# The first pair of tiles in eight plain block products, with the weight sums made meanwhile

## The chip, the cores and the metric

One Trainium2 chip, one core. The metric is the device time of one execution in microseconds, as the median of several runs. Lower is better.

## The reference

A layer of an encoder on x of 2048 rows by 1024 columns: RMS norm, a gated linear attention mixer, residual, RMS norm, a gated convolutional feed-forward part, residual, final norm, all in float32.

```python
h = rmsnorm(x, mix_norm_w)
proj = h @ w_in                       # q, k, v, r, and 16 columns glr
q, k, v, r, glr = split(proj)
log_a = log_sigmoid(glr @ w_gate2 + b_gate) / 16
# chunks of 64 rows: state = state * decay + k_decayed^T v ; o = q state
o = rms_normalize(o) * gla_norm_w * silu(r)
x = x + o @ w_out
h = rmsnorm(x, ffn_norm_w)
u = causal_dwconv(h @ w_up, conv_w, conv_b); g, val = split(u)
x = x + (silu(g) * val) @ w_down
return rmsnorm(x, final_norm_w)
```

The change touches the start of `h @ w_in`: the 1024 columns of r (called "R" in the kernel) and the gate's 16 columns glr, for the first two row tiles.

## The kernel before

**Numbers.** A float32 operand a is held as a rounded high part and a remainder, a = hi + lo (`split`: a ScalarE cast at L185 makes hi, a VectorE subtraction at L186 makes lo). A product takes three matmuls (L178 to L180): hi·lo, lo·hi, hi·hi.

**Tiles.** The rows are taken in pairs of tiles, 2 x 128 rows. For a pair j and a group of 1024 weight columns ("R", then "A", "B", "Y"), `unit` computes a 2 x 2 block product: rows b(e), b(d), each in two halves of 512 along the inner dimension, times four weight blocks of 512 x 512. It does so with seven products instead of eight (the Strassen-Winograd scheme): p1, p5, p6, p7, p4, p2, p3. Each is 4 inner steps x 3 matmuls = 12 matmuls of 128 x 512. Weight blocks (i, j) are named by column half i and inner half j. p5 takes the sum of blocks (1,0) and (1,1), p6 that sum minus (0,0), p7 (0,0) minus (1,0), p3 (0,1) minus p6's sum; p1, p4 and p2 take (0,0), (1,1) and (0,1). On the row side, p5, p6, p7 and p4 take differences of the pair's blocks (`ht` tiles, made by `diff`). The split weights stay in tiles `w_R_p1` and so on for all eight pairs.

**A row tile's way.** `load_x` (SyncE's queue), `norm_x` (ScalarE square into `junk`, VectorE variance `var_a`, GpSimd power `rstd_a`, VectorE scaling), `blocks_x` (eight transposes on TensorE into two banks `pt_a`, two copies into `hb`), differences, split, store to DRAM (`h1d`) for the later groups.

**Order.** Each engine runs its instructions in the order in which the code issues them. The host code keeps a clock (`adv`) that products advance; `later_do(us, fn)` and the list `wevents` issue work when that clock passes a time. For the first pair the order was written out: the table `WEARLY` says how many weight products are prepared before product i, and `limit` how many rows. All sums and splits of weights for p1 to p3 are issued inside the first pair's `unit`, each ahead of its product. The blocks (0,0), (1,0) and (1,1) come by `stage_w` into tiles that later hold split weights, block (0,1) by ScalarE's queue into tiles `wr`.

**The gate.** `gate_weights` loads the 16 gate columns (`graw`), the second gate matrix and the bias (`w2raw`, eight small loads) on ScalarE's queue and splits them on VectorE (`wg`, `w2s`). `gate_mm` adds the gate's matmuls (into `pg`) to four of the seven products.

**Banks.** The eight PSUM banks are two pools of four: "mm" (products, `pg`) and "aux" (transposes and others). A tile of a pool waits until the last reader of the bank that it gets has ended.

Of the kernel before, what the change touches and what calls it, by code (L numbers as in the profile page):

```python
# [20 lines left out]
def f32(ap):  # L21
    return ap.bitcast(F32)
# [3 lines left out]
def hybrid_kernel(  # L26
# [48 lines left out]
    TB0, TB1, TB2 = 4.0, 10.0, 3.0  # L75
    TX0, TX = (16.4, 18.6), (10.8, 13.5)

# [158 lines left out]
    WSUM = ("p5", "p6", "p7", "p3")  # L236
    wgot, wload, staged = {}, {}, {}

# [41 lines left out]

    def stage_w(ps_, o, ijs):

        t = uh.tile([P, KT, 512], F32, tag=o, name=f"ws_{ps_}_{o}", bufs=1)
        for n, ij in enumerate(ijs):
            for c, src in w_block(ps_, *ij):
                nc.sync.dma_start(t[:, n * HK:(n + 1) * HK, c:c + src.shape[-1]], src)
            staged[ij] = t[:, n * HK:(n + 1) * HK, :]

    def raws_of(ps_, o, k):
        v = (slice(None), slice(2 * k, 2 * k + 2))  # L290
        return v, [wgot[ps_, o, k, ij] if (ps_, o, k, ij) in wgot else staged[ij][v] for ij in WSRC[o]]

    def sum_w(ps_, o, k):

        v, r = raws_of(ps_, o, k)
        src = xsum[v]
        if o == "p5":
            nc.vector.tensor_add(src, *r)
        elif o == "p6":
            nc.vector.tensor_sub(src, src, r[0])  # L300
        elif o == "p7":
            nc.vector.tensor_sub(r[1], *r)
        elif o == "p3":
            r = wgot[ps_, "p2", k, (0, 1)] if (ps_, "p2", k, (0, 1)) in wgot else staged[0, 1][v]
            nc.vector.tensor_sub(src, r, src)
# [91 lines left out]
    def blocks_x(t):  # L397
        xt = xin.pop(t)
        bs = []
        for k in range(2):  # L400
            pt = aux_ps(f"pt_a{t}_{k}")
            for i in range(HK):
                kt = HK * k + i
                nc.tensor.transpose(pt[:, i * P:(i + 1) * P], xt[:, kt * P:(kt + 1) * P], ident)
            b = hb_tile(f"hb_{t}_{k}")
            nc.vector.tensor_copy(b, pt)
            bs.append(b)
        hsrc["t", t] = bs
        j = t // 2
        if t % 2 == 0:  # L410
            hsrc[j, "p1"], hsrc[j, "p2"] = bs
            return
# [51 lines left out]
    def gate_weights():  # L464

        GR = 2 * RANK
        rp["wg"] = wg = rp["p"].tile([P, 2, KT, GR], F32R, name="wg")
        graw = rp["p"].tile([P, 512], F32, tag="s2k", name="graw", bufs=SB)
        gv = graw[:, :KT * RANK].rearrange("p (a b) -> p a b", b=RANK)
        nc.scalar.dma_start(gv, wv[:, :, OR + H * DV:OR + H * DV + RANK])  # L470
        nc.gpsimd.memset(f32(wg[:, 1, :, RANK:GR]), 0.0)
        nc.vector.tensor_copy(wg[:, 0, :, :RANK], gv)
        nc.vector.tensor_copy(wg[:, 1, :, :RANK], gv)
        nc.vector.tensor_sub(wg[:, 0, :, RANK:GR], gv, f32(wg[:, 0, :, :RANK]))


        rp["w2s"] = w2s = rp["p"].tile([P, 512], F32R, name="w2s")
        w2raw = rp["p"].tile([P, 512], F32, tag="s2k", name="w2raw", bufs=SB)
        for i in range(6):
            nc.scalar.dma_start(w2raw[i * RANK:(i + 1) * RANK, :], w_gate2)  # L480
        for i in range(2):
            nc.scalar.dma_start(w2raw[96 + i:97 + i, :], b_gate)
        nc.vector.tensor_copy(w2s[0:98, :], w2raw[0:98, :])
        for r in (slice(64, 96), slice(96, 98)):
            nc.vector.tensor_sub(w2s[r, :], w2raw[r, :], f32(w2s[r, :]))
        nc.vector.tensor_copy(w2s[96:97, :], w2raw[96:97, :])
        rp["gstk"] = rp["p"].tile([P, T], F32R, name="gstk")
        nc.gpsimd.memset(f32(rp["gstk"][96:98, :]), 1.0)

    def gate_mm(j, o, hh, hl):  # L490
# [17 lines left out]
        if o == "p3":  # L508
            sl = slice(j % 2 * 256, j % 2 * 256 + 256)
            g = rp["gstk"]  # L510
            nc.scalar.copy(g[0:GR, sl], pg[:GR, :256])
            nc.vector.tensor_sub(g[GR:2 * GR, sl], pg[:GR, :256], f32(g[0:GR, sl]))
            nc.scalar.copy(g[2 * GR:3 * GR, sl], pg[:GR, :256])
            ready.add(f"g{j}")
            if j % 2 == 1:
                gates(j // 2, TB0, TB1, TB2)

# [339 lines left out]
    ux = {}  # L857
    WEARLY = [0, 2, 3, 4, 5, 6, 7, 7]

    def limit(ps_, j, i):  # L860

        own = (PS.index(ps_) * NP + j + 1) * len(PORD)
        n = own - len(PORD) + i + 1 + LEAD
        if ps_ == "R" and j == 0 and i < len(PORD) - 2:
            return min(n, i + 2)
        if ps_ == "R" and j + 1 < NP:
# [3 lines left out]
    def unit(ps_, j):  # L870
# [5 lines left out]
        bank, keep = {}, {}  # L876
        first = ps_ == "R" and j == 0
        if ps_ == "R":
            if first:
                wload[ps_] = len(WHALF) - 2  # L880
                load_w(ps_, len(WHALF))
            elif j + 2 < NP:
                for t in (e + 4, d + 4):
                    xin[t] = load_x(t, "x")
            if j + 1 < NP:
                for i, t in enumerate((e + 2, d + 2)):
                    norm_x(t)
                    later_do((TX0 if first else TX)[i], lambda t=t: blocks_x(t))

# [388 lines left out]
    masks()  # L1278
    nc.gpsimd.memset(halo, 0.0)
# [123 lines left out]
```

## Time and profile before

| | |
|---|---|
| median of 3 runs | 2235.53 us (2234.98 to 2243.4) |
| profiled execution | 2241.04 us, span 2238.9 us |
| TensorE busy | 2126.9 us, 95% of the span |
| VectorE, ScalarE, GpSimd busy | 73%, 49%, 33% |
| TensorE busy, 0 to 26 us | 4.37 us |
| VectorE busy, 26 to 61 us | 32.91 us of 35 |
| second pair starts on TensorE | 60.87 us |
| third pair starts on TensorE | 86.27 us |

Busy time is summed over instructions; an idle time stands with the event that ended it. The trace's rows give start, length, engine, line, operation, output and inputs, all in microseconds from the span's start. PE is TensorE, PEld its weight load, DVE VectorE, ACT ScalarE, POOL GpSimd, SP SyncE; a q behind the name is the engine's queue of DMA issues.

### The profile page before, as it was taken

Reading aid. Unit: us, or ns where it says so; the run is one execution under the profiler, and the core shown is the slowest. Engines: PE = TensorE matmul, PEld = TensorE weight load, DVE = VectorE, ACT = ScalarE, POOL = GpSimd, SP = SyncE. Lnnn points to the kernel's source line nnn. Section 1 sums busy time; section 2 is a strip of 40 time slices with the busy share of each in tenths; the row PEclk is TensorE's granted clock in tenths of the full one; section 3 lists DMA queues with packets and bytes.
Section 4 is the critical chain, followed back from the end, with each engine's and each line's share of the span. In section 5 each row is a group of like instructions: output and inputs, shape, how many; then the busy total and the mean of one; then the engine's idle time right before and its main releaser. Section 6 shows DMA issues by size and latency. Waiting matters only on the chain.

```text
span 2238.9 us, 29122 instructions
## 1 busy us (share of the span) xinstructions
PE 2126.9 (95%) x9948; PEld 1741.8 (78%) x9948; DVE 1642.1 (73%) x2175; ACT 1107.5 (49%) x2020; POOL 729.1 (33%) x602
## 2 busy tenths in 40 slices
PE   5999999989999899899999999999999999999998
PEld 3788787877887787677787778788888888888886
DVE  7755777788778765388999787797877777557564
ACT  4554655565555576445445444444444543333342
POOL 1000111112111000265566565466655535046100
PEclk9999999999999999999999999999999999999999
DMA  6545684369546799943535428624242468454443
GB/s 209 195 156 185 206 294 126 123 198 325 169 160 196 266 318 335 364 137 123 189 127 163 147 90 282 192 76 136 71 141 71 136 230 321 137 183 151 141 171 116
DMA packets 305077, 411.78 MB, mean 184 GB/s; under 512 B 23694, under 2 KB 160062, under 8 KB 304928
## 3 DMA queue, kind: packets, MB, share of 16 engines
q1 hardware_dynamic: 266156, 346.72, 46.6%
q10 hardware_dynamic: 38772, 63.20, 8.4%
q8 instruction: 78, 1.28, 0.2%
q14 instruction: 71, 0.58, 0.1%
HBM read 266.70 MB, written 143.13 MB: 183 GB/s over the span
## 4 chain that ended last, share of the span: by engine, by line
PE 62%; DVE 14%; DMA 9%; issue 5%; ACT 5%; POOL 3%; SPq 1%; ACTq 0%; DVEq 0%; POOLq 0%
PE pd_p L179 5%; PE pd_p L180 5%; PE pd_p L178 5%; PE ua L178 5%; PE ua L179 5%; PE ua L180 5%; DVE t L1078 4%; PE mp_R L178 2%; PE uc L178 2%; PE uc L180 2%; PE uc L179 2%; PE mp_R L179 2%; PE mp_R L180 2%; DVE uw_p L186 2%; PE mp_A L178 1%
## 5 line engine op out<-in xcount | busy, mean ns | idle before, releaser
L178 PE MATMUL ua<-h_p,uw_p 128*128 128x512 f32 x704 | 280.4, 398 | 24.3 <-ACT c L1060 24.3
L179 PE MATMUL ua<-h_p,uw_p 128*128 128x512 f32 x704 | 278.9, 396 | 0.0
L180 PE MATMUL ua<-h_p,uw_p 128*128 128x512 f32 x704 | 278.5, 396 | 0.0
L1078 DVE SCALAR_TENSOR_TENSOR t<-u,cw,t 128x1024 f32<-128x1024 f32 x176 | 264.2, 1505 | 8.6 <-ACT t L1076 7.5
L179 PE MATMUL pd_p<-dw_p,da 128*128 128x512 f32 x616 | 240.1, 390 | 1.1 <-DVE da L186 1.1
L180 PE MATMUL pd_p<-dw_p,da 128*128 128x512 f32 x616 | 239.9, 389 | 0.0
L178 PE MATMUL pd_p<-dw_p,da 128*128 128x512 f32 x616 | 239.9, 389 | 0.0
L186 DVE TENSOR_TENSOR uw_p<-ur,uw_p 128x512 fp32r<-128x512 f32 x176 | 168.4, 973 | 59.4 <-ACT uw_p L185 52.3
L186 DVE TENSOR_TENSOR da<-da_p,da 128x512 fp32r<-128x512 f32 x154 | 135.6, 933 | 100.5 <-ACT da L185 99.4
L185 ACT CAST da<-da_p 128x512 fp32r<-128x512 f32 x154 | 85.2, 619 | 203.8 <-PE pd_p L180 149.9
L178 PEld LDWEIGHTS ua<-h_p,uw_p 128*128 128x128 f32 x704 | 134.3, 191 | 58.1 <-ACT c L1060 28.6
L185 ACT CAST uw_p<-us 128x512 fp32r<-128x512 f32 x132 | 82.1, 622 | 164.5 <-POOL us L1040 114.1
L186 DVE TENSOR_TENSOR uw_p<-us,uw_p 128x512 fp32r<-128x512 f32 x132 | 122.4, 936 | 53.4 <-ACT uw_p L185 53.0
L180 PEld LDWEIGHTS ua<-h_p,uw_p 128*128 128x128 f32 x704 | 134.2, 191 | 29.9
L179 PEld LDWEIGHTS ua<-h_p,uw_p 128*128 128x128 f32 x704 | 134.4, 191 | 29.4
L178 PE MATMUL uc<-h_p,uw_p 128*128 128x512 f32 x352 | 138.4, 393 | 0.7 <-DMA h_p<-hd_p 0.7
L179 PE MATMUL uc<-h_p,uw_p 128*128 128x512 f32 x352 | 138.1, 392 | 0.0
L180 PE MATMUL uc<-h_p,uw_p 128*128 128x512 f32 x352 | 138.1, 392 | 0.0
L179 PEld LDWEIGHTS pd_p<-dw_p,da 128*128 128x128 f32 x616 | 115.7, 188 | 25.9 <-DVE da L186 1.9
L1076 ACT ACTIVATE t<-u,cw 128x1024 f32<-128x1024 f32 x88 | 109.7, 1247 | 50.9 <-DVE u L1169 43.0
L178 PEld LDWEIGHTS pd_p<-dw_p,da 128*128 128x128 f32 x616 | 115.7, 188 | 24.2
L180 PEld LDWEIGHTS pd_p<-dw_p,da 128*128 128x128 f32 x616 | 115.7, 188 | 23.7
(251 smaller groups left out, 5477.8 us busy)
## 6 DMA issues: line engine op xcount, KB each, us to landing
ur<-in_ffn_w_up_dram SPq DMA_DIRECT2D x168, 256.0 KB, 3.7
da_p<-ad_p SPq DMA_DIRECT2D x154, 256.0 KB, 3.8
h_p<-hd_p SPq DMA_DIRECT2D x56, 512.0 KB, 7.6
ad_p<-as_p SPq DMA_DIRECT2D x88, 256.0 KB, 2.5
ad_p<-t SPq DMA_DIRECT2D x66, 256.0 KB, 3.2
x<-in_x_dram SPq DMA_DIRECT2D x32, 512.0 KB, 4.9
ch<-in_ffn_w_down_dram SPq DMA_DIRECT2D x61, 256.0 KB, 4.0
hr_A_p<-h1d_p SPq DMA_DIRECT2D x56, 256.0 KB, 2.7
```

The costliest lines, as they stand in the source:

```text
L178: nc.tensor.matmul(ps_ap, ah, bl, start=(first and i == 0), stop=False, **kw)
L179: nc.tensor.matmul(ps_ap, al, bh, start=False, stop=False, **kw)
L180: nc.tensor.matmul(ps_ap, ah, bh, start=False, stop=(last and i == len(pairs) - 1), **kw)
L185: nc.scalar.copy(hi, src)
L186: nc.vector.tensor_sub(lo, src, f32(hi))
L1076: nc.scalar.activation(t, u[:, 2:2 + TS], AF.Identity, scale=cw[:, 2, c:c + 1], bias=cw[:, 3, c:c + 1])
L1078: nc.vector.scalar_tensor_tensor(t, u[:, k:k + TS], cw[:, k, c:c + 1], t, op0=ALU.mult, op1=ALU.add)
```

## The change

The first pair of "R" no longer goes through `unit`. A new function `first_pair` computes it as eight plain products (2 column halves x 2 row tiles x 2 inner halves, 96 matmuls instead of 84), each of which needs only a weight block as it comes and a row block as it is transposed. Results are accumulated in four banks and copied out by ScalarE. The sums for p5, p6, p7 and p3 are issued during these products and used by the second pair first. The pair's own row differences, which only later groups read, are issued 22 us of the host clock later. The copies of the transposes of tiles 2 and 3 go from VectorE to ScalarE. The gate's loads go from ScalarE's queue to SyncE's, behind the weight blocks, and its split of `w2raw` comes 44 us of the host clock later. `wgot` replaces the staged blocks, and `stage_w`, `WEARLY` and the special cases of the first pair are removed.

```diff
-    TX0, TX = (16.4, 18.6), (10.8, 13.5)
+    TX = (10.8, 13.5)
...
 def blocks_x(t):
-            b = hb_tile(f"hb_{t}_{k}")
-            nc.vector.tensor_copy(b, pt)
+            if t < 2:
+                b = rp["p"].tile([P, 512], F32, tag="s2k", name=f"hb_{t}_{k}", bufs=SB)
+            else:
+                b = hb_tile(f"hb_{t}_{k}")
+            (nc.scalar.copy if t in (2, 3) else nc.vector.tensor_copy)(b, pt)
...
 def gate_weights():
-        nc.scalar.dma_start(gv, wv[:, :, OR + H * DV:OR + H * DV + RANK])
+        nc.sync.dma_start(gv, wv[:, :, OR + H * DV:OR + H * DV + RANK])
...
+    def gate_weights2():
-            nc.scalar.dma_start(w2raw[i * RANK:(i + 1) * RANK, :], w_gate2)
+            nc.sync.dma_start(w2raw[i * RANK:(i + 1) * RANK, :], w_gate2)
...
+        later_do(44.0, parts)
...
+    def first_pair():
...
+        fetch((0, 0), (1, 0))
+        gate_weights()
+        xin[2], xin[3] = load_x(2, "x"), load_x(3, "x")
+        fetch((1, 1))
+        gate_weights2()
+        for t in range(2):
+            norm_x(t)
+            blocks_x(t)
...
+        def sum5():
+            for k in range(2):
+                nc.vector.tensor_add(s_[V[k]], a21[V[k]], a22[V[k]])
+            split_sum("p5", [s_[V[k]] for k in range(2)])
+        def sum6():
+            for k in range(2):
+                nc.vector.tensor_sub(s_[V[k]], s_[V[k]], a11[V[k]])
+            for k in range(2):
+                nc.vector.tensor_sub(xsum[V[k]], a11[V[k]], a21[V[k]])
+            split_sum("p6", [s_[V[k]] for k in range(2)])
+        def sum7():
+            for k in range(2):
+                nc.vector.tensor_sub(a12[k], a12[k], s_[V[k]])
+            split_sum("p7", [xsum[V[k]] for k in range(2)])
...
+        def product(i, jj, k):
+            if jj == 0:
+                bank[i, k] = (aux_ps if (i, k) == (1, 1) else mm_ps)(f"m{i}{k}_{ps_}_{j}")
+            (hh, hl), (wh, wl) = h[jj, k], w[i, jj]
...
+            mm3p(bank[i, k], pairs, first=(jj == 0), last=(jj == 1))
+            if jj == 1:
+                t = out_tile(f"o{i}{k}_{ps_}_{j}")
+                nc.scalar.copy(t, bank[i, k])
+                nc.sync.dma_start(rd[k][i], t)
+        weight("p1", (0, 0), "p1")
+        row(0, 0)
+        row(0, 1)
+        weight("p3", (1, 0))
+        product(0, 0, 0)
+        gate_plain(j, 0, 0, *h[0, 0])
+        row(1, 0)
+        product(0, 0, 1)
+        gate_plain(j, 0, 1, *h[0, 1])
+        weight("p4", (1, 1), "p4")
+        row(1, 1)
+        for k in range(2):
+            r = raw_tile([P, 2, 512], f"wr_{ps_}_{k}")
+            load_block(nc.scalar, r, ps_, k, (0, 1))
+            a12.append(r)
+        need_raw[0, 1] = a12
+        product(1, 0, 0)
+        norm_x(2)
+        norm_x(3)
+        product(1, 0, 1)
+        weight("p2", (0, 1), "p2")
+        product(1, 1, 0)
+        gate_plain(j, 1, 0, *h[1, 0])
+        blocks_x(2)
+        blocks_x(3)
+        product(1, 1, 1)
+        gate_plain(j, 1, 1, *h[1, 1])
+        done["rows"] = len(PORD)
+        prep_rows(len(PORD) + 1)
+        sum5()
+        product(0, 1, 0)
+        prep_rows(len(PORD) + 2)
+        sum6()
+        product(0, 1, 1)
+        later_do(22.0, diffs)
+        for t in (4, 5):
+            xin[t] = load_x(t, "x")
+        heapq.heappush(wevents, (clock["now"] + 1.0, next(seq), sum7))
+        heapq.heappush(wevents, (clock["now"] + 5.0, next(seq), lambda: split_sum("p3", a12)))
...
-    gate_weights()
...
-    stage_w("R", "p2", ((0, 0), (1, 0)))
-    stage_w("R", "p3", ((1, 1),))
-    xin[2], xin[3] = load_x(2, "x"), load_x(3, "x")
-    for t in range(2):
-        norm_x(t)
-        blocks_x(t)
+    first_pair()
...
-        for j in range(NP):
+        for j in range(int(ps_ == "R"), NP):
             unit(ps_, j)
```

What stands where in the built program, at the places that matter. A row gives line, operation, output and inputs with their buffer numbers, and shape; `x2` means two such rows. The number after `x_`, `hb_` or `pt_a` is the row tile; `ws_p7` is the staged block (0,0), `ws_p6` blocks (1,1) and (1,0); `w_R_p1` and `w_R_p3` hold, in the first pair of the changed kernel, the split blocks (0,0) and (1,0).

SyncE's queue at the start. Before:

```order
L377 DMA x_0_537<-in_x_dram 128x1024
L1270 DMA nw_mix_539<-in_mix_norm_w_dram 128x1024
L377 DMA x_1_541<-in_x_dram 128x1024
L286 DMA ws_R_p2_543<-in_gla_w_in_dram 128x4x512 x2
L286 DMA ws_R_p3_546<-in_gla_w_in_dram 128x4x512
L377 DMA x_2_548<-in_x_dram 128x1024
L377 DMA x_3_550<-in_x_dram 128x1024
```

SyncE's queue at the start. After:

```order
L369 DMA x_0_514<-in_x_dram 128x1024
L1420 DMA nw_mix_516<-in_mix_norm_w_dram 128x1024
L369 DMA x_1_518<-in_x_dram 128x1024
L899 DMA ws_p7_520<-in_gla_w_in_dram 128x2x512 x2
L899 DMA ws_p6_521<-in_gla_w_in_dram 128x2x512 x2
L467 DMA graw_527<-in_gla_w_in_dram 128x8x16
L369 DMA x_2_533<-in_x_dram 128x1024
L369 DMA x_3_535<-in_x_dram 128x1024
L899 DMA ws_p6_521<-in_gla_w_in_dram 128x2x512 x2
L479 DMA w2raw_540<-in_gla_w_gate2_dram 16x512 x6
L481 DMA w2raw_540<-in_gla_b_gate_dram 1x512 x2
```

The weight blocks come in half blocks, and the gate's loads, which stood first on ScalarE's queue, now stand here behind them.

VectorE, from its first instruction behind the gate's first casts. Before:

```order
L483 CAST w2s_521<-w2raw_522 98x512
L485 TENSOR_TENSOR w2s_521<-w2raw_522,w2s_521 32x512
L485 TENSOR_TENSOR w2s_521<-w2raw_522,w2s_521 2x512
L206 TENSOR_SCALAR var_a0_555<-ssq_a0_553 128x1
L486 CAST w2s_521<-w2raw_522 1x512
L386 SCALAR_TENSOR_TENSOR x_0_537<-x_0_537,rstd_a0_557,nw_mix_539 128x1024
L206 TENSOR_SCALAR var_a1_577<-ssq_a1_575 128x1
L186 TENSOR_TENSOR w_R_p1_636<-ws_R_p2_543,w_R_p1_636 128x1024
L386 SCALAR_TENSOR_TENSOR x_1_541<-x_1_541,rstd_a1_579,nw_mix_539 128x1024
L406 COPY hb_0_0_565<-pt_a0_0_560 128x512
```

VectorE, from the norm of tile 0. After:

```order
L378 SCALAR_TENSOR_TENSOR x_0_514<-x_0_514,rstd_a0_556,nw_mix_516 128x1024
L378 SCALAR_TENSOR_TENSOR x_1_518<-x_1_518,rstd_a1_578,nw_mix_516 128x1024
L186 TENSOR_TENSOR w_R_p1_608<-ws_p7_520,w_R_p1_608 128x1024 x2
L186 TENSOR_TENSOR w_R_p3_620<-ws_p6_521,w_R_p3_620 128x1024
L469 CAST wg_526<-graw_527 128x8x16
L470 CAST wg_526<-graw_527 128x8x16
L471 TENSOR_TENSOR wg_526<-graw_527,wg_526 128x8x16
L186 TENSOR_TENSOR w_R_p3_620<-ws_p6_521,w_R_p3_620 128x1024
L955 TENSOR_TENSOR xsum_507<-ws_p7_520,ws_p6_521 128x1024 x2
L401 COPY hb_0_0_564<-pt_a0_0_559 128x512
```

The `w2s` steps are gone from here (they stand behind the sum for p5 now), and the first copy of a transposed block stands behind four weight splits and the difference for p7.

ScalarE, around the end of the first pair (`o` tiles are results, `m` and `mp` banks of products). Before:

```order
L974 COPY o21_R_0_805<-mp1_R_0_656 128x512
L204 ACTIVATE junk_5_927,ssq_a5_928<-x_5_887 128x1024
L185 CAST w_R_p3_809<-xsum_507 128x1024 x2
L185 CAST h_R1_p1_853<-hb_2_0_824 128x512
L185 CAST h_R1_p5_881<-ht_1_p5_847 128x512
```

After:

```order
L185 CAST w_R_p5_821<-ws_p7_520 128x1024 x2
L185 CAST w_R_p6_849<-ws_p7_520 128x1024 x2
L185 CAST w_R_p3_948<-wr_R_0_681 128x1024
L985 COPY o10_R_0_744<-m10_R_0_685 128x512
L401 COPY hb_2_0_760<-pt_a2_0_755 128x512
L401 COPY hb_2_1_767<-pt_a2_1_762 128x512
L401 COPY hb_3_0_774<-pt_a3_0_769 128x512
L401 COPY hb_3_1_781<-pt_a3_1_776 128x512
L185 CAST h_R1_p1_815<-hb_2_0_760 128x512
```

The copies of tiles 2 and 3 now stand on ScalarE behind the casts for p5, p6 and the first half of p3.

More of the change, by code (lines that the diff above doesn't have):

```diff
@@ L279, in make_sums @@
             later_do(8.0 + 3.0 * i, lambda st=st: step(*st))
[L281 to L287, printed above, removed]
     def raws_of(ps_, o, k):
         v = (slice(None), slice(2 * k, 2 * k + 2))
-        return v, [wgot[ps_, o, k, ij] if (ps_, o, k, ij) in wgot else staged[ij][v] for ij in WSRC[o]]
+        return v, [wgot[ps_, o, k, ij] for ij in WSRC[o]]
     def sum_w(ps_, o, k):
@@ L508, in gate_mm, with gate_rows @@
         if o == "p3":
[L509 to L516, printed above, removed]
+            gate_rows(j)
+    def gate_rows(j):
+        GR = 2 * RANK
+        pg = rp["pg"]
+        sl = slice(j % 2 * 256, j % 2 * 256 + 256)
+        g = rp["gstk"]
+        nc.scalar.copy(g[0:GR, sl], pg[:GR, :256])
+        nc.vector.tensor_sub(g[GR:2 * GR, sl], pg[:GR, :256], f32(g[0:GR, sl]))
+        nc.scalar.copy(g[2 * GR:3 * GR, sl], pg[:GR, :256])
+        ready.add(f"g{j}")
+        if j % 2 == 1:
+            gates(j // 2, TB0, TB1, TB2)
     def gates(b, t0, t1, t2):
@@ L876, in unit @@
         bank, keep = {}, {}
-        first = ps_ == "R" and j == 0
         if ps_ == "R":
[L879 to L882, printed above, removed]
+            if j + 2 < NP:
                 for t in (e + 4, d + 4):
@@ L887, in unit @@
                     norm_x(t)
-                    later_do((TX0 if first else TX)[i], lambda t=t: blocks_x(t))
+                    later_do(TX[i], lambda t=t: blocks_x(t))
         def out(src, other, name):
```

105 lines of the change are left out of this document (82 added, 23 removed).

## The prediction

> **What bounds the kernel now.** I read the page first (who is busy over the whole run), then the busy time of each engine in the stretches of the program's start, then the waits there, then the timelines. From the page, and from the stretches (columns: PE, weight load, VectorE, ScalarE, GpSimd busy; granted clock; DMA share; GB/s):
>
> ```profile
> PE 2126.9 (95%) x9948; PEld 1741.8 (78%) x9948; DVE 1642.1 (73%) x2175; ACT 1107.5 (49%) x2020; POOL 729.1 (33%) x602
> 0.00:26.00 26.00, 4.37 (x17) 3.46 (x18) 13.09 (x25) 9.23 (x14) 4.39 (x18) 1.00 0.88 292
> 26.00:61.00 35.00, 28.59 (x144) 21.99 (x144) 32.91 (x38) 19.10 (x25) 2.92 (x2) 0.95 0.48 156
> 61.00:86.00 25.00, 24.06 (x137) 19.27 (x136) 21.66 (x36) 10.26 (x19) 2.85 (x4) 1.00 0.64 225
> 110.00:140.00 30.00, 29.98 (x182) 24.77 (x181) 16.94 (x27) 11.46 (x24) 1.41 (x2) 1.00 0.50 178
> ```
>
> TensorE bounds the run as a whole, but not its first 61 us. Up to 26 us it is idle but for 4.4 us, and the DMA engines are 88% busy; from 26 to 61 us, the first pair of tiles, VectorE is busy 32.9 of 35 us and bounds. From the second pair on TensorE has no room left (29.98 of 30). So whatever start the third pair gets, the rest of the program keeps: its instructions stand in the same order before and after. The first waits:
>
> ```profile
> ACT L204 <- DMA w2raw<-in_gla_w_gate_dram: 9.0, 1, 9.0
> DVE w2s L483 <- DMA ws_R_p<-in_gla_w_in_dram: 6.6, 1, 6.6
> PE pt_a L404 <- DVE var_a L206: 16.8, 1, 16.8
> SPq L286 <- DMA w2raw<-in_gla_w_gate_dram: 6.2, 2, 4.9
> ```
>
> The gate's small loads hold three queues: ScalarE issues nothing else until 9.0 us, SyncE starts the weight blocks only after them, and VectorE, in order, stands at `w2s` before the first norm. TensorE's marks (start, length, instruction, idle time before it):
>
> ```profile
> 26.00 0.79 PE L179 MATMUL mp_R<-w_R_p,h_R_p 128*128 128x512 f32 x1 [3.90 <-DVE var_a L206]
> 42.37 0.44 PE L568 MATMUL pt_c<-ident,rows 44*128 44x44 f32 x4
> 42.74 1.53 PE L404 MATMUL pt_a<-ident,x 128*128 128x128 f32 x12
> ...
> 60.87 0.45 PE L178 MATMUL mp_R<-w_R_p,h_R_p 128*128 128x512 f32 x1
> 62.24 0.50 PE L179 MATMUL mp_R<-w_R_p,h_R_p 128*128 128x512 f32 x1 [0.92 <-DVE h_R_p L186]
> ...
> 65.90 0.47 PE L178 MATMUL mp_R<-w_R_p,h_R_p 128*128 128x512 f32 x1
> 68.75 0.22 PE L505 MATMUL pg<-h_R_p,wg 128*32 128x128 f32 x1
> 69.23 0.46 PE L178 MATMUL mp_R<-w_R_p,h_R_p 128*128 128x512 f32 x1
> 86.27 0.46 PE L178 MATMUL mp_R<-w_R_p,h_R_p 128*128 128x512 f32 x1
> ```
>
> Streaming begins at 26.00, the second pair at 60.87, the third at 86.27. A product of 12 matmuls takes 65.90 to 68.75, 2.85 us; eight gate matmuls 0.48; twelve transposes about 1.3.
>
> **Step 1, loads.** The gate's loads leave ScalarE's queue and go behind the weights on SyncE's. Rates:
>
> ```profile
> 0.00:2.50 2.50, 0.00 (x0) 0.00 (x0) 0.00 (x0) 0.00 (x0) 1.74 (x13) 1.00 0.24 48
> 2.50:5.00 2.50, 0.00 (x0) 0.00 (x0) 0.00 (x0) 0.00 (x0) 0.46 (x4) 1.00 1.06 302
> 10.00:12.50 2.50, 0.00 (x0) 0.00 (x0) 0.00 (x0) 2.49 (x6) 0.00 (x0) 1.00 1.04 379
> 47.66:48.18 0.52, 0.05 (x1) 0.05 (x1) 0.52 (x3) 0.00 (x0) 0.00 (x0) 1.00 0.00 0
> ```
>
> Tile 0, the norm weights and tile 1 are 3 x 524 KB = 1.57 MB. By 5.0 us 0.12 + 0.755 MB have come; the rest at 379 GB/s takes 1.84 us, to 6.85. The last row is the gap between the last byte of a tile's load and the ScalarE instruction that waited for it at 48.19 (below): 0.5 us. So tile 1 is usable at 7.4; bounds 6.9 (the full rate from 2.5 us) and 8.3 (today's mix). The four half blocks follow at 1.38 each, the last byte at 12.4; ScalarE needs it by 14. The small loads end some 10 us before VectorE now wants them (rival 4).
>
> **Step 2, VectorE to the first product.** Durations:
>
> ```profile
> 5.17 0.23 DVE L472 CAST wg<-graw 128x128 fp32r<-128x128 f32 x1 [5.17 <-DMA graw<-in_gla_w_in_dram]
> 16.64 0.15 DVE L206 TENSOR_SCALAR var_a<-ssq_a 128x1 f32<-128x1 f32 x1
> 18.37 1.28 DVE L386 SCALAR_TENSOR_TENSOR x<-x,rstd_a,nw_mix 128x1024 f32<-128x1024 f32 x1 [0.45 <-POOL rstd_a L208]
> 34.58 2.36 DVE L300 TENSOR_TENSOR xsum<-xsum,ws_R_p 128x1024 f32<-128x1024 f32 x2
> 36.85 0.69 DVE L186 TENSOR_TENSOR h_R_p<-ht_p,h_R_p 128x512 fp32r<-128x512 f32 x1
> 37.45 2.36 DVE L186 TENSOR_TENSOR w_R_p<-xsum,w_R_p 128x1024 fp32r<-128x1024 f32 x2
> 58.50 2.48 DVE L406 COPY hb<-pt_a 128x512 f32<-128x512 f32 x4
> 66.92 2.48 DVE L386 SCALAR_TENSOR_TENSOR x<-x,rstd_a,nw_mix 128x1024 f32<-128x1024 f32 x2 [0.44 <-POOL rstd_a L208]
> ```
>
> Start to start, a weight half costs 1.135, a row 0.60, a norm 1.20, a copy 0.60. Square 1.1 (11.35 row below) from 7.4 gives 8.5; from variance to norm 1.73 (16.64 to 18.37): tile 1's norm starts at 10.3, today 18.37. From there VectorE never starves: norm 1.20, four weight halves 4.54, three `wg` casts 0.5, `xsum` 2.27, four copies 2.39, two mask casts 0.3, the low part of the first row 0.69: 11.9. Streaming begins at 22.2, 3.8 us earlier than 26.00. The copies stand behind six weight-sized operations, where before none stood between tile 1's norm and them; that is why 8 us become 3.8. ScalarE's two weight loads for block (0,1) stand ahead of the squares of tiles 2 and 3; tile 3's last byte comes at about 15.5 by the same rate, so the squares end by 18, before the first copy does at 19.4: hidden.
>
> **Step 3, VectorE and ScalarE to the second pair's transposes.** The four copies of tiles 2 and 3 move to ScalarE, where they stand behind the cast of the third difference's block (`w_R_p3`), which waits for VectorE's L960. VectorE up to L960: rows 1.8, weight halves 2.27 + 1.135 + 1.135, variances 0.15, two norms 2.4 plus waits for GpSimd 0.75, sum 2.27, `w2s` 0.45, split 2.27, difference 2.27, L960 1.135: 18.0, so 40.2. ScalarE, with the issue of a tile's load on SyncE:
>
> ```profile
> 11.35 1.04 ACT L204 ACTIVATE junk<-x 128x1024 bf16<-128x1024 f32 x1
> 44.99 2.00 ACT L185 CAST w_R_p<-wr_R 128x1024 fp32r<-128x1024 f32 x2 [1.34 <-DVE w_R_p L186]
> 43.86 0.33 SPq L377 DMA_DIRECT2D x<-in_x_dram  x1
> 48.19 1.06 ACT L204 ACTIVATE junk<-x 128x1024 bf16<-128x1024 f32 x1 [1.20 <-DMA x<-in_x_dram]
> 53.43 0.58 ACT L974 COPY o_R<-mp_R 128x512 f32<-128x512 f32 x1 [2.55 <-PE mp_R L180]
> ```
>
> Cast 1.0, product copy 0.5, tile copy 0.6: 42.3. The fourth group of transposes needs that copy, since the fourth bank of their pool holds product (1,1).
>
> **Step 4, TensorE.** By then it has 58 matmuls (13.8), 24 gate matmuls (1.4) and 12 transposes (1.3): 22.2 + 16.5 = 38.7 at full clock. It starts cold, however:
>
> ```profile
> 32.16:35.58 3.42, 1.26 (x4) 0.86 (x5) 3.42 (x4) 0.42 (x1) 0.00 (x0) 1.00 0.34 126
> 35.58:38.99 3.41, 3.41 (x10) 2.50 (x9) 3.41 (x5) 2.09 (x2) 0.00 (x0) 0.51 0.00 0
> 45.82:49.23 3.41, 1.87 (x10) 1.08 (x8) 2.85 (x5) 2.21 (x4) 0.00 (x0) 1.00 0.40 155
> ```
>
> A stretch of 3.41 us at clock 0.51 costs 1.7. One such, and TensorE is there at 40.4 and waits 1.9 (bounds 0 to 2.5). Then four transposes 0.4, a product and its gate 3.33, two products 5.7: the second pair starts at 51.75, 9.1 earlier. The eighth product (+2.85) and eight gate matmuls fewer (-0.48) are in this. ScalarE still copies four results out of the banks, VectorE no longer adds three (1.8); the pair's own four differences (2.4 on VectorE) go into the second pair, and their stores on SyncE come behind the loads of tiles 4 to 7, so they delay none: cost 0 as long as VectorE has its room there. In the second pair the 0.92 stall goes: its first row's low part is ready at 47.9 (40.2 plus four weight halves, 4.54, and five row-sized operations, 3.1). `pt_c` comes in, +0.37. Third pair: 86.27 - 9.1 - 0.92 + 0.37 = 76.6. **Sum: 9.65 us gained.** The profiled execution took 2241.04 us (span 2238.9 plus 2.1), 5.5 above the median; against its own time 2231.4, against the median of 2235.53 2225.9.
>
> What is late next: ScalarE's square of tile 5 (rival 3). What hides the sums of p7 and p3: TensorE's p1, p5 and p6, 51.75 to about 62; VectorE finishes the last split at about 54 (47.9 plus three weight halves, a norm and the row-sized rest). If that cover went, p7 and p3 would wait for them.
>
> The clock, weighed. Row: 1.26 of 3.42 us busy was followed by half clock, 1.87 was not, so 1.7 to 2 us idle in one stretch suffices. The Trainium skill, "TensorE: Matmul & The Clock Gate", HAM oscillation, warns of gaps over about 3.4 us; by that the 1.9 us wait is harmless and the sum stays 2225.9. The trace disagrees with it: 2.16 idle were enough.
>
> **Rivals.**
> 1. *Clock.* The wait of 1.9 falls into one stretch and the next runs at half: 1.7 lost, 2227.6. It takes the wait near its upper end and a stretch that doesn't cut it. Chance 0.22.
> 2. *Shorter chain.* GpSimd's power took from 0.5 to 1.5 us:
>
> ```profile
> L208 POOL TENSOR_TENSOR rstd_a<-var_a,neghalf x8: 544/890/1465, 14.7 to 81.1; 128x1 f32<-128x1 f32 x8
> DMA to landing us min/median/max: 3.5/5.8/9.7
> ```
>
> With short ones the chain loses 0.9 before the first norm and 0.75 later, and the copy at 42.3 comes at 40.7; TensorE, 0.9 earlier too, arrives at 39.5 and still waits for it: gain 11.3, 2224.2. For it speaks the median of 0.9 in that row; against it the 1.73 from variance to norm at 16.64, beside a busy VectorE as now. Chance 0.22.
> 3. *Tile 5 late.* Its load is issued behind VectorE's difference at 45.3. Landing in 4.3 us (43.86 to 48.19 before) it is hidden; in 9.7, the longest above, ScalarE stands until 56.6, and its copy that frees the bank of p5 ends at 57.4 (two small copies after it), while TensorE wants the bank at 55.6 (51.75 plus a product and two gates): 1.8 lost, 2227.7. Chance 0.08.
> 4. *Slower.* `w2s` now stands on VectorE before the split of p5's weights and waits for eight small loads at the end of SyncE's start. They must land by 34.0; the last issue is free at about 22, landing by 27. Each us after 34.0 is lost whole: at 43.7 nothing is gained, at 55 it is 0.5% slower, 2247. Against it: 7 us of room. Chance 0.03.
>
> **How the numbers follow.** My case 0.40; what I don't see 0.05. The forecast is 2225.9. The cases lie between 2224.2 and 2227.7, tile 1's bounds add 0.5 below and 0.9 above, and the runs shown reach from 0.6 below their median to 7.9 above: 2219 to 2233. The line of 0.5% (11.2 us, about what a measurement of this kernel can tell from no change) lies at 2224.3: rival 2 ends on it, and the rest within. Faster 0.28, same 0.68, slower 0.04.
>
> **What would show it.** First full product at about 22.2, ScalarE's first square at 4 to 5 us, a TensorE wait of 0 to 2.5 us before the fourth transposes with ScalarE as releaser, second pair at 51.75, third at 76.6, no new wait after. Wrong if TensorE waits in the second pair for ScalarE or VectorE, or if VectorE starves before 40 us.

## The result: 2225.76 us, and the profile after

| | before | after |
|---|---|---|
| median of 9 runs | 2235.53 us (2233.04 to 2245.4) | 2225.76 us (2223.8 to 2230.0) |
| ratio, 95% interval | | 0.9948 (0.9935 to 0.9961) |
| span of the profiled execution | 2238.9 us | 2225.9 us |
| first full product / second pair / third pair on TensorE | 26.00 / 60.87 / 86.27 | 22.75 / 52.30 / 76.74 |

The gain of 9.77 us between the medians is 0.44%. The ratio says 0.52%, which is 11.6 us, with an interval of 8.7 to 14.5 us: clear of zero, and on both sides of the line of 0.5%. Single executions of some variants below, among them the profiled one of e3, ran at a mean granted clock of 0.21 to 0.85 and are left out of every comparison. The page of the changed kernel, its busy line:

```profile
PE 2122.0 (95%) x9952; PEld 1739.3 (78%) x9952; DVE 1635.3 (73%) x2167; ACT 1110.3 (50%) x2023; POOL 729.8 (33%) x602
```

TensorE's marks after, from its timeline (start, length, instruction, idle time before it and what ended it):

```profile
21.29 0.79 PE L178 MATMUL m_R<-w_R_p,h_R 128*128 128x512 f32 x1 [6.65 <-ACT h_R L185]
22.75 0.79 PE L178 MATMUL m_R<-w_R_p,h_R 128*128 128x512 f32 x1 [0.67 <-ACT h_R L185]
...
26.81 0.52 PE L178 MATMUL m_R<-w_R_p,h_R 128*128 128x512 f32 x1
27.17 0.40 PE L179 MATMUL m_R<-w_R_p,h_R 128*128 128x512 f32 x1
...
39.93 1.48 PE L396 MATMUL pt_a<-ident,x 128*128 128x128 f32 x12
43.02 0.65 PE L396 MATMUL pt_a<-ident,x 128*128 128x128 f32 x4 [1.61 <-ACT hb L401]
52.30 0.39 PE L178 MATMUL mp_R<-w_R_p,h_R_p 128*128 128x512 f32 x1
...
76.74 0.46 PE L178 MATMUL mp_R<-w_R_p,h_R_p 128*128 128x512 f32 x1
```

The reader is to see three things: products run at half speed until about 27.1 (0.43 us from start to start, then 0.23); one wait of 1.61 us ahead of the fourth group of transposes, ended by ScalarE's copy into `hb`; and a third pair 9.53 us earlier than before. The two profiled spans differ by 13.0; the other 3.47 lie behind the third pair, where the order is the same: there the traces' clock records show 17 stretches of 3.41 us at half clock before and 15 after (without the one at the end of each trace), and two of them cost up to 3.41 us together where TensorE is busy throughout. So this part is put down to the clock and not to the change, which no run shows apart. The medians (9.77) don't have it; the interval of the ratio would allow it.

VectorE, GpSimd and ScalarE on the way to that wait:

```profile
11.32 1.28 DVE L378 SCALAR_TENSOR_TENSOR x<-x,rstd_a,nw_mix 128x1024 f32<-128x1024 f32 x1 [0.45 <-POOL rstd_a L208]
12.52 3.58 DVE L186 TENSOR_TENSOR w_R_p<-ws_p,w_R_p 128x1024 fp32r<-128x1024 f32 x3
...
17.64 2.34 DVE L955 TENSOR_TENSOR xsum<-ws_p,ws_p 128x1024 f32<-128x1024 f32 x2
19.91 2.47 DVE L401 COPY hb<-pt_a 128x512 f32<-128x512 f32 x4
...
34.77 0.42 DVE L483 CAST w2s<-w2raw 98x512 fp32r<-98x512 f32 x1
...
39.64 1.22 DVE L960 TENSOR_TENSOR wr_R<-wr_R,ws_p 128x1024 f32<-128x1024 f32 x1
```

```profile
9.71 1.58 POOL L208 TENSOR_TENSOR rstd_a<-var_a,neghalf 128x1 f32<-128x1 f32 x1 [3.03 <-DVE var_a L206]
```

```profile
8.29 1.06 ACT L204 ACTIVATE junk<-x 128x1024 bf16<-128x1024 f32 x1 [2.64 <-DMA x<-in_x_dram]
...
40.95 1.04 ACT L185 CAST w_R_p<-wr_R 128x1024 fp32r<-128x1024 f32 x1
41.90 0.58 ACT L985 COPY o_R<-m_R 128x512 f32<-128x512 f32 x1
42.38 2.06 ACT L401 COPY hb<-pt_a 128x512 f32<-128x512 f32 x4
```

### The profile page after: what moved, and what is told of

It reads as the page before. It is cut to its first block, busy times and chain, and to the rows that moved or that the text cites. A ratio compares the mean times of both kernels' runs of the same rounds, so it can differ in the third digit from the quotient of the medians.

```text
span 2225.9 us, 29128 instructions
## 1 busy us (share of the span) xinstructions
PE 2122.0 (95%) x9952; PEld 1739.3 (78%) x9952; DVE 1635.3 (73%) x2167; ACT 1110.3 (50%) x2023; POOL 729.8 (33%) x602
## 4 chain that ended last, share of the span: by engine, by line
PE 40%; DVE 9%; DMA 6%; issue 4%; ACT 3%; POOL 3%; SPq 0%; ACTq 0%; DVEq 0%; POOLq 0%
PE pd_p L179 5%; PE pd_p L180 5%; PE pd_p L178 5%; PE ua L178 5%; PE ua L180 5%; PE ua L179 5%; DVE t L1229 4%; PE uc L178 2%; PE uc L180 2%; PE uc L179 2%; DVE uw_p L186 2%; DMA xs<-x1d 1%; PE ub L180 1%; PE ub L178 1%; PE ub L179 1%
```

## The experiments

A median moves with the half-clock stretches of the whole run, and its interval is some 0.2% (4 us) to each side; the start of the third pair in the profile is the same to 0.01 us in two profiles of the changed kernel. So the variants are compared by that mark, with VectorE's busy and idle time up to it (busy time in the stretch from 0 to the mark; idle is the rest). For any engine the two add up to the mark; that VectorE's are the ones that count is for the runs to show.

| kernel | first product | second pair | third pair | VectorE busy + idle | ratio to before |
|---|---|---|---|---|---|
| before | 26.00 | 60.87 | 86.27 | 67.94 + 18.33 | 1 |
| changed | 22.75 | 52.30 | 76.74 | 64.07 + 12.67 | 0.9948 (0.9935 to 0.9961) |
| changed, again (e23) | 22.61 | 52.14 | 76.74 | 64.18 + 12.56 | 0.9961 (0.9945 to 0.9977) |
| e1 gate's loads alone | 19.89 | 54.09 | 80.37 | 67.64 + 12.73 | 0.9983 (0.997 to 0.9996) |
| e2 products alone | 22.76 | 49.87 | 78.86 | 64.13 + 14.73 | 0.9973 (0.9956 to 0.9989) |
| e3b tile 3 later | 22.67 | 50.50 | 76.68 | 64.09 + 12.59 | 0.9937 (0.9915 to 0.9958) |
| e4 18 unread matmuls | 22.46 | 51.78 | 76.58 | 64.11 + 12.47 | 0.9952 (0.9934 to 0.9969) |
| e9 28 unread matmuls | 22.73 | 53.60 | 78.38 | 64.27 + 14.11 | 0.9964 (0.9947 to 0.998) |
| e10 both of these | 22.66 | 48.67 | 77.00 | 64.03 + 12.97 | 0.9967 (0.995 to 0.9984) |
| e11 difference on GpSimd | 24.91 | 54.46 | 78.92 | 66.14 + 12.78 | 0.9946 (0.9927 to 0.9965) |
| e18 difference left out | 20.41 | 49.98 | 74.46 | 61.81 + 12.65 | 0.9938 (0.9922 to 0.9954) |
| e21 four edits | 23.89 | 50.91 | 79.61 | 61.97 + 17.64 | 0.9948 (0.9929 to 0.9967) |
| e7 two edits | 20.14 | 47.50 | 77.72 | 63.91 + 13.81 | 0.995 (0.9931 to 0.9969) |

Among the variants, e2, e7, e9, e10 and e21 have one stretch of 3.41 us at half clock between the cold start and the third pair (from 63.22, 68.18, 42.91, 55.10 and 58.10 us); the others have none there. Where it weighs is said with each.

**The two parts.** e1 is the kernel before with this alone:

```diff
-        nc.scalar.dma_start(gv, ...)          # and the eight of w2raw
+        nc.sync.dma_start(gv, ...)
...
-    gate_weights()
     xin[0] = load_x(0, "x")
...
     stage_w("R", "p2", ((0, 0), (1, 0)))
+    gate_weights()
     stage_w("R", "p3", ((1, 1),))
     xin[2], xin[3] = load_x(2, "x"), load_x(3, "x")
+    gate_weights2()                           # its parts by later_do(44.0, parts)
```

> One part alone: the kernel before, in which only the gate's loads go to SyncE's queue, behind the weight blocks, and the split of w2raw comes later. Theory A (VectorE's chain from tile 1's norm bounds the first pair, and the gate's loads only delay its start): tile 1's norm comes at 11 to 12 instead of 18.37 us, three w2s steps (some 2 us) leave the chain, and the third pair starts at 78 to 81 instead of 86.27; median 2228 to 2231, so the larger part of the change's gain lies here. Theory B (the arrival of the weight blocks sets the pace, DMA share 0.88 up to 26 us, so that the eight plain products bring the gain): third pair at 84 to 86, median 2233 to 2235.

e2 is the changed kernel with the opposite: both calls first in the program, on `nc.scalar`, and nothing of the gate on SyncE's queue.

> The other part alone: the changed kernel with the gate's loads back on ScalarE's queue, first in the program. Theory A: tile 1's norm is back at about 18, the second pair starts 6 to 7 us later than in the changed kernel (at 58 to 59.5), the third at 82.5 to 84 instead of 76.74; median 2231 to 2233. Theory B: the third pair starts at 77 to 80, median 2226 to 2229.

The stretch up to the third pair, of before, of the changed kernel, of e1 and of e2 (columns as in the prediction's stretches):

```profile
0.00:86.27 86.27, 57.29 (x300) 44.99 (x301) 67.94 (x96) 38.59 (x58) 10.16 (x24) 0.98 0.65 217
```

```profile
0.00:76.74 76.74, 56.80 (x304) 46.19 (x305) 64.07 (x88) 41.04 (x61) 11.62 (x24) 1.00 0.70 241
```

```profile
0.00:80.37 80.37, 56.95 (x301) 44.19 (x301) 67.64 (x96) 38.68 (x58) 11.09 (x24) 0.96 0.68 234
```

```profile
0.00:78.86 78.86, 57.38 (x305) 46.81 (x305) 64.13 (x88) 40.18 (x61) 11.52 (x24) 0.98 0.68 227
```

The third number is VectorE's. Of the 9.53 us, 3.87 are work taken off VectorE and 5.66 are idle time taken off it. e1 has the idle part almost alone (0.30 work, 5.60 idle): tile 1's norm stands at 11.00 instead of 18.37. e2 has the work part (3.81) and 3.60 less idle. So by the mark theory A was right on e1 (80.37, expected 78 to 81) and wrong on e2 (78.86, expected 82.5 to 84); the medians, 2234.46 and 2233.27 beside 2238.16 for the kernel before in the same session, lie above what was expected of e1 (2228 to 2231) and just above A's for e2 (2231 to 2233). On e2 I had shifted the whole chain by the late norm, but e2's order differs. There the copies follow tile 1's norm (16.73) at once and the weight splits come behind them, so that the first product is at 22.76 as in the changed kernel, and the splits are missing later:

```profile
17.93 1.98 DVE L401 COPY hb<-pt_a 128x512 f32<-128x512 f32 x3
...
49.87 0.39 PE L178 MATMUL mp_R<-w_R_p,h_R_p 128*128 128x512 f32 x1
...
63.74 0.80 PE L178 MATMUL mp_R<-w_R_p,h_R_p 128*128 128x512 f32 x1 [2.83 <-ACT cp_R L1107]
```

The first of these rows is VectorE's, the others TensorE's. e2 starts its second pair 2.43 us before the changed kernel and its third 2.12 after it. The wait of 2.83 us goes back to VectorE: ScalarE, whose copy of a product (`cp_R`) ends it, had itself stood 4.38 us until VectorE's difference `ht_p` of 60.81.

**Is it the wait?** e3, the only wait removed:

```diff
         blocks_x(2)
-        blocks_x(3)
         product(1, 1, 1)
         gate_plain(j, 1, 1, *h[1, 1])
+        blocks_x(3)
```

> The changed kernel with the transposes of tile 3 moved behind product (1,1), so that TensorE has work while ScalarE copies the first transposed block of tile 2. Theory A (the 1.61 us wait before the fourth group of transposes is TensorE's only loss between 23 us and the third pair): the wait is gone, second pair at 50.7, third pair 1.2 to 1.7 earlier, at 75.0 to 75.5; median 1 to 2 lower than the changed kernel's. Theory B (VectorE's rows for the second pair, whose third row's low part ends at 57.4 against its product at 59.26, are the next limit): the wait comes back inside the second pair, third pair at 76.2 to 76.8.

> The same kernel as e3_tile3_later once more, for a profile at full clock. Theory A: no wait at the transposes of tiles 2 and 3, second pair at 50.7, third pair at 75.0 to 75.5. Theory B: the wait comes back inside the second pair before its third product, third pair at 76.2 to 76.8.

e3 and e3b are one kernel, run in two sessions (ratios 0.9933, 0.9914 to 0.9951, and 0.9937). The rows are e3b's:

```profile
50.50 0.39 PE L178 MATMUL mp_R<-w_R_p,h_R_p 128*128 128x512 f32 x1
55.71 0.50 PE L179 MATMUL mp_R<-w_R_p,h_R_p 128*128 128x512 f32 x1 [1.08 <-DVE var_a L206]
...
76.68 0.46 PE L178 MATMUL mp_R<-w_R_p,h_R_p 128*128 128x512 f32 x1
```

The wait is gone and the second pair starts 1.8 us earlier, but the third doesn't (76.68): VectorE's low parts for the second and third products end at 55.65 and 56.32, and TensorE waits for them (`var_a` in the row is the small instruction between the two). It waits once more at 67.99, for VectorE's first sum of results. Theory B: 1.80 won, 1.74 lost. The wait for ScalarE's copy was not what cost 1.6 us; it was where VectorE's lateness showed first.

**Is it TensorE's cold start?** e4 and e9 put 18 and 28 matmuls, whose result nobody reads, into the gap before the first product:

```diff
         weight("p1", (0, 0), "p1")
+        warm = mm_ps("warm")
+        for _ in range(18):                   # e9: 28
+            nc.tensor.matmul(warm, w[0, 0][1][:, 3, :P], w[0, 0][1][:, 3, :], start=True, stop=True)
```

> The changed kernel with 18 extra matmuls of 128x512 on TensorE between the last transposes (14.6) and the first product (21.3), whose result nobody reads, so that the granted clock is full when the products start. Theory A (TensorE waits for ScalarE's copy anyway): the products from 22.75 run at 0.23 instead of 0.43 us a matmul, TensorE is at the transposes of tile 2 about 2 us earlier, waits about 3.7 instead of 1.61 and the third pair starts where it did, 76.7 (within 0.3), unless the long wait brings a stretch of half clock, then 78.4. Theory B (TensorE's own work bounds the first pair): third pair 2 us earlier, at 74.7.

> As e4_warm, but with 28 unread matmuls instead of 18: the 18 ended at 19.75, left TensorE idle for most of the 3.41 us before 23.0, and the products up to 26.4 ran at half clock again. Now they reach to about 22. Theory A (TensorE waits for ScalarE's copy anyway): the products run at 0.23 us a matmul from the start, TensorE is at the transposes of tile 2 at 39.2 to 39.6 instead of 41.41, waits 3.3 to 3.7 there, and the third pair starts at 76.4 to 76.9; if the wait brings half clock, at 78. Theory B (TensorE's own work bounds the first pair): third pair at 74.5 to 75.

e4's 18 ended at 19.75; the stretches behind it, and those around e9's wait, with the wait ahead of them (columns as before; the granted clock stands behind GpSimd's busy time):

```profile
19.63:23.05 3.42, 1.21 (x4) 0.48 (x3) 3.42 (x9) 2.72 (x5) 0.00 (x0) 0.99 0.87 234
23.05:26.46 3.41, 3.41 (x8) 2.70 (x9) 3.41 (x5) 3.25 (x4) 0.00 (x0) 0.51 0.56 207
```

```profile
42.75 1.01 PE L396 MATMUL pt_a<-ident,x 128*128 128x128 f32 x4 [3.09 <-ACT hb L401]
```

```profile
39.49:42.91 3.42, 0.33 (x3) 0.17 (x2) 3.42 (x4) 3.39 (x6) 0.00 (x0) 1.00 0.33 86
42.91:46.32 3.41, 3.41 (x11) 2.83 (x11) 3.41 (x5) 3.12 (x6) 0.00 (x0) 0.50 0.88 285
```

e4 didn't warm the products, and its third pair came at 76.58. In e9 they ran at full clock from 22.73, TensorE was at the transposes at 39.66 instead of 41.41, waited 3.09 instead of 1.61 for the same copy, and lost a half-clock stretch behind it: third pair at 78.38. Theory A. The cold start costs 2.2 us on TensorE and nothing on the path. The second profile of the changed kernel, e23, shows the same without an edit: there the clock is 0.50 until 28.34, TensorE waits 0.97 instead of 1.61, and the third pair starts at the same 76.74.

e10 has both edits.

> The changed kernel with both edits, the transposes of tile 3 behind product (1,1) and 28 unread matmuls ahead of the first product. Theory A: what the warm clock gives is no longer lost in the wait for ScalarE's copy, but the rows of the second pair on VectorE (third row's low part at 57.4) then set the pace: second pair at 48.6 to 49, a wait of 1 to 2 before its third product, third pair at 74 to 75. Theory B (nothing else in the way): third pair at 73.2 or earlier. Theory C (the edits don't add, TensorE isn't what bounds): 75.0 to 75.5 as with the transposes alone.

```profile
48.67 0.39 PE L178 MATMUL mp_R<-w_R_p,h_R_p 128*128 128x512 f32 x1
53.08 0.49 PE L178 MATMUL mp_R<-w_R_p,h_R_p 128*128 128x512 f32 x1 [0.20 <-ACT o_R L985]
54.88 0.63 PE L179 MATMUL mp_R<-w_R_p,h_R_p 128*128 128x512 f32 x1 [1.31 <-DVE var_a L206]
```

The second pair starts 3.6 us earlier than in the changed kernel, the third at 77.00, later than any of the three theories said: the wait for VectorE comes back inside the pair. A second thing comes with it, a stretch at half clock behind the wait:

```profile
51.69:55.10 3.41, 1.86 (x18) 1.38 (x19) 3.41 (x7) 2.54 (x5) 0.13 (x1) 1.00 0.62 201
55.10:58.51 3.41, 3.41 (x9) 2.66 (x9) 2.94 (x5) 0.67 (x2) 0.80 (x1) 0.50 0.99 378
```

How much each takes can be read at VectorE's first sum of results in the second pair, `o_R`, for which e3b's weight load stands 0.57 us until 67.99. Its rows in the changed kernel, e3b, e10 and (below) e7:

```profile
67.32 0.68 DVE L1054 TENSOR_TENSOR o_R<-mp_R,cp_R 128x512 f32<-128x512 f32 x1
67.26 0.68 DVE L1054 TENSOR_TENSOR o_R<-mp_R,cp_R 128x512 f32<-128x512 f32 x1
67.19 0.68 DVE L1057 TENSOR_TENSOR o_R<-mp_R,cp_R 128x512 f32<-128x512 f32 x1
66.70 0.68 DVE L1054 TENSOR_TENSOR o_R<-mp_R,cp_R 128x512 f32<-128x512 f32 x1
```

The third pair starts 8.74 us after the end of this row in the changed kernel and in e3b, and 8.77 to 8.81 after it in e2, e11 and e18. In e10 it is 9.13, so that the half clock costs some 0.4 us (an estimate), and VectorE alone would have put the mark at 76.6.

**Is it VectorE?** e18 takes the p7 difference off VectorE's queue, by leaving it out; e11 puts it on GpSimd.

```diff
             for k in range(2):
-                nc.vector.tensor_sub(xsum[V[k]], a11[V[k]], a21[V[k]])
+                nc.gpsimd.tensor_sub(xsum[V[k]], a11[V[k]], a21[V[k]])      # e11; not there in e18
...
-            split_sum("p7", [xsum[V[k]] for k in range(2)])
+            split_sum("p7", a12)                                             # e18
```

> The changed kernel without the two difference rows for p7 (2.27 us on VectorE ahead of the first copies); the split for p7 takes the weights of p3 instead, so the products of p7 are left wrong; the order is otherwise the same on TensorE, ScalarE and VectorE. Theory A (VectorE's chain from tile 1's norm to the second pair's rows sets the third pair's start, one for one; the waits of TensorE only show where it surfaces): first full product at 20.5, last difference L960 2.2 earlier, second pair at 50.0 to 50.4, third pair 2.0 to 2.3 earlier than the changed kernel's, at 74.4 to 74.8. Theory B (TensorE's half-clock start, its wait for ScalarE's copy or the loads set it): less than 1 earlier, 75.7 or later.

```profile
20.41 0.80 PE L178 MATMUL m_R<-w_R_p,h_R 128*128 128x512 f32 x1 [0.67 <-ACT h_R L185]
40.68 0.66 PE L396 MATMUL pt_a<-ident,x 128*128 128x128 f32 x4 [0.95 <-ACT hb L401]
49.98 0.39 PE L178 MATMUL mp_R<-w_R_p,h_R_p 128*128 128x512 f32 x1
...
74.46 0.46 PE L178 MATMUL mp_R<-w_R_p,h_R_p 128*128 128x512 f32 x1
```

```profile
0.00:74.46 74.46, 57.51 (x304) 46.56 (x305) 61.81 (x86) 41.13 (x61) 11.61 (x24) 1.00 0.75 247
```

> The changed kernel with the difference for p7 (two halves, 2.27 us on VectorE ahead of the first copies of transposed blocks) on GpSimd, which is idle there; the order on the other engines is the same. GpSimd's rows of 128x512 take 1.55 to 1.75, so two of 128x1024 some 6.4, from 12.4 to 19, with the masks behind them to 20.6. Theory A (VectorE's chain sets both the first product and, by the last difference and ScalarE's copies, the wait): first full product at 20.5 to 21.1 instead of 22.75, the difference L960 2 us earlier, the wait about the same 1.5, second pair at 50.0 to 50.6, third at 74.5 to 75.1; median 1.6 to 2.3 below the changed kernel's. Theory B (GpSimd's work slows VectorE's beside it, or the masks come late): VectorE's 128x1024 rows from 12 to 19 get longer than their 1.2, the product comes no earlier than 22, third pair at 76 or later.

VectorE's row of three weight splits and GpSimd's two differences in e11:

```profile
12.63 7.90 DVE L186 TENSOR_TENSOR w_R_p<-ws_p,w_R_p 128x1024 fp32r<-128x1024 f32 x3
```

```profile
12.56 5.66 POOL L955 TENSOR_TENSOR xsum<-ws_p,ws_p 128x1024 f32<-128x1024 f32 x2 [1.17 <-DMA ws_p<-in_gla_w_in_dram]
```

With 2.26 us less VectorE work (61.81 against 64.07) and the same order, the third pair is 2.28 earlier, as theory A had it. In e11 (theory B) the same three splits take 7.90 instead of 3.58 beside GpSimd, VectorE ends up 2.07 busier, and the third pair is 2.18 later. In both directions one for one. This is shown; that TensorE's waits and cold start don't count is shown by e3b, e9, e10 and e23 (e4 left the products cold and decides nothing).

**A better version?** e21 and e7 keep all the work and change the order on VectorE; the build can place an instruction whose inputs are there ahead of its place in the code (the difference of `sum6` runs at 17.64), so an order has to be read from the built program.

```diff
-            for k in range(2):                 # sum6; e7 and e21
-                nc.vector.tensor_sub(xsum[V[k]], a11[V[k]], a21[V[k]])
...
+            for k in range(2):                 # sum7
+                nc.vector.tensor_sub(xsum[V[k]], a22[V[k]], s_[V[k]])
...                                             # blocks_x(3) as in e3; e7 and e21
-            (nc.scalar.copy if t in (2, 3) else nc.vector.tensor_copy)(b, pt)
+            (nc.scalar.copy if t < 4 else nc.vector.tensor_copy)(b, pt)      # e21, and masks() ahead of the norms
```

> A try at a better version: the changed kernel with the first four copies (2.39 us) on ScalarE too, the difference for p7 made from p6's sum behind the other sums, the masks first and tile 3's transposes behind product (1,1). VectorE loses 2.4 us of work, but the norms of tiles 2 and 3 now stand ahead of its first rows. Theory A (VectorE's amount of work counts): third pair at 75.0 to 75.9 although the first product comes as late as 23 to 23.5. Theory B (the first product's time counts): third pair at 76.7 or later.

> The changed kernel once more, unaltered, beside the two above on the same chip: a second look at its first 90 us and its spread. Third pair again at 76.7 within 0.4; median 8 to 11 below the kernel before.

> A version meant to beat both: the changed kernel with the difference for p7 made as block (1,1) minus p6's sum, so that it can't stand ahead of the first copies on VectorE, and with tile 3's transposes behind product (1,1). Nothing is taken off VectorE; its work is only put into the order in which TensorE needs it. Theory A (VectorE's chain to each thing that TensorE waits for, worked out along the new order with the changed kernel's durations: first full product at 20.5, TensorE at tile 2's transposes 39.1, no wait there, second pair at 49.3, its second row's low part at 51.2 against a use at 53.0, its third at 54.2 against 56.2): third pair at 73.5 to 74.5, 2.2 to 3.2 earlier than the changed kernel's 76.74. Theory B (VectorE's amount of work up to the second pair counts, whatever the order): 76.3 to 76.8.

```profile
23.89 0.79 PE L179 MATMUL m_R<-w_R_p,h_R 128*128 128x512 f32 x1 [1.76 <-DVE h_R L186]
55.67 0.50 PE L178 MATMUL mp_R<-w_R_p,h_R_p 128*128 128x512 f32 x1 [0.92 <-ACT o_R L985]
57.48 0.50 PE L179 MATMUL mp_R<-w_R_p,h_R_p 128*128 128x512 f32 x1 [1.30 <-DVE h_R_p L186]
```

```profile
47.50 0.39 PE L178 MATMUL mp_R<-w_R_p,h_R_p 128*128 128x512 f32 x1
...
59.66 0.50 PE L178 MATMUL mp_R<-w_R_p,h_R_p 128*128 128x512 f32 x1 [1.09 <-ACT cp_R L1109]
...
67.44 0.50 PE L178 MATMUL mp_R<-w_R_p,h_R_p 128*128 128x512 f32 x1 [2.17 <-DVE o_R L1054]
```

```profile
64.77:68.18 3.41, 1.24 (x6) 0.71 (x5) 3.28 (x6) 0.00 (x0) 0.44 (x1) 1.00 0.80 216
68.18:71.59 3.41, 3.41 (x9) 2.65 (x9) 3.41 (x7) 0.00 (x0) 0.40 (x1) 0.50 1.02 387
```

The rows are TensorE's of e21 and then of e7, and the last two are stretches of e7. Neither beats the changed kernel by its mark; e23, the changed kernel again, came as expected (76.74, its median 9.8 us below that of the kernel before). e7 starts the second pair 4.8 us earlier, 1.8 earlier than worked out, and gives more than that back, to two things. I had followed the rows of three products and not the results behind them, whose sums (`o_R`) VectorE also makes, late: the first ends at 67.38, only 0.62 earlier than in the changed kernel, and TensorE stands 2.17 us for it. And behind this wait TensorE runs at half clock, so that the third pair starts 10.34 us after the sum instead of 8.74. Without the half clock the mark would be some 76.1 (an estimate: 67.38 + 8.74). e21 has 2.1 us less VectorE work and 5 us more idle: the norms of tiles 2 and 3 stand ahead of the first rows, the waits above follow, behind them comes the half clock from 58.10, and VectorE then waits 1.85 us itself for transposes that TensorE makes late. So the amount of work on VectorE bounds the mark only as long as nothing leaves VectorE idle, and a wait on TensorE costs more than itself where half clock follows. Theory A failed in both: in e7 the new order brought VectorE's first sum little forward, in e21 the order cost more than the work saved. The ratios of e3 and e3b are the lowest of the complete kernels, but their intervals overlap the changed kernel's, and e3b's mark says no gain; that it is faster isn't shown.

## Why the prediction was right, step by step

- **Step 1, loads.** Tile 1 was usable at 8.3, the upper bound given (8.29, its square), not 7.4: the term was 0.9 too small. `w2s` found its small loads there (34.77, no wait): rival 4 had room.
- **Step 2.** The norm came at 11.32, not 10.3: the 0.9, and a power of 1.58 us, so rival 2's short one was not on the path. From norm to first product 11.4 us against 11.9 worked out; the first product came at 22.75, not 22.2. The reading that four weight halves and the `xsum` rows ahead of the copies eat the earlier start is confirmed by e18: without `xsum`, 20.41.
- **Step 3.** L960's first half ended at 40.86 against 40.2, ScalarE's copy at about 43.0 (TensorE goes on at 43.02) against 42.3: the two casts and copies behind it as worked out.
- **Step 4.** TensorE was there at 41.41, not 40.4: 0.55 from the start, the rest from the cold products, 4.3 us at half speed, which cost 2.2, not 1.7 (the granted clock reads 1.00 in this trace's rows up to there, and the distance of the matmuls shows it; in e23 the clock is 0.50 from 18.10 to 28.34). The wait was 1.61 against 1.9; second pair at 52.30 against 51.75. The second pair then took 24.44 us against 24.85 worked out, so the third came at 76.74 against 76.6; half of that 0.41 is that the stall of 0.92 in the second pair before had cost 1.14 (60.87 to 62.24, where a matmul takes 0.23). Rival 3's place shows no wait.
- **The sum.** 9.65 predicted, 9.53 at the third pair, 9.77 between the medians. Errors of 0.5 to 1.0 in the marks were nearly cancelled by the 0.41 in the second pair, and by TensorE waiting for the chain whenever it arrived. That 2225.9 meets the median of 2225.76 so closely is therefore luck.
- **Rival 1, the clock.** The wait left 1.80 of 3.41 us busy and full clock followed. e9 shows the rival's mechanism at 0.33: half clock, and 1.64 us lost at the third pair. In e10 half clock followed a stretch with 1.86, so that 1.55 us idle can be enough, less than the 1.7 to 2 that the prediction read from its two rows (1.54 wasn't enough, 2.16 was); that the changed kernel escapes is in part luck.
- **What the prediction had wrong though its number was right.** It treated the wait of 1.9 as TensorE's loss, and put the pair's own four differences at "cost 0 as long as VectorE has its room there". They did cost nothing here, since TensorE streams through the second pair without a gap; but VectorE has no room: from 45 to 62 us it is busy 15.80 of 17. Its first sum of results ends at 68.00, about when TensorE needs it. e3b, e10 and e7 show that time won before the second pair is lost in it, to VectorE's rows and this sum, and in e7 to the half clock behind the wait for the sum. The right reading is one bound, VectorE's work and idle time up to the second pair's rows and first sum; the change pays by the work that it takes off VectorE (3.87) and by the idle time (5.66, of which 2.97 lies ahead of tile 1's norm and 2.69 behind it).

## What to carry to other kernels

Where an engine is busy almost without a gap through two stages, add up its busy and idle time to the point from which the rest is fixed: a change gains what it takes off either, and a wait removed on the engine behind it only moves. Look at the clock in each trace before you compare: a wait that half clock follows costs more than itself. Try the parts alone, since their gains (5.90 and 7.41 here) need not add up to the whole (9.53). To test whether an engine bounds, leave out one of its operations and keep the order: if it bounds, the mark moves by about what the operation took (2.28 for 2.26 here).

## What the runs showed of the hardware that I had not expected

- VectorE and GpSimd hold each other up on these operations: beside 5.66 us of GpSimd's subtractions (both inputs in SBUF), VectorE's three subtractions took 7.90 instead of 3.58, 4.3 of the 5.66 lost. The Trainium skill, "SBUF — State Buffer", Who interferes with whom, says that the two share a port pair by an exclusive lock and that a VectorE instruction with two SBUF inputs contends with a GpSimd instruction that reads SBUF; the trace agrees, though not for the whole time: by these numbers some 1.3 us of the two ran side by side (an estimate).
- Half clock followed a stretch of 3.41 us with 0.33 (e9), 1.20 (e4) or 1.24 us (e7) of TensorE work, and full clock one with 1.80 (the changed kernel). But half clock followed one with 1.86 (e10) too, so that the busy time of the stretch doesn't settle it alone; what else counts stays open. In e9 the gap was 3.09 us, under the 3.4 of the rule that the prediction weighed ("TensorE: Matmul & The Clock Gate", the Trainium skill), and in e10 the longest was 1.31; the trace disagrees with it here too.
- Unread matmuls kept the clock up here only where they reached to the work: 18 that ended 2.7 us before the first product left it at half clock, 28 that ended at 21.9 didn't.
